# State space tables from factors that are transposed once, outputs in front of the next batch, and loads for sums requested one gate block ahead

## The chip, the cores and the metric

The kernel runs on one core of one Trainium2 chip. The metric is the device time of one execution in microseconds (us). The kernel before took 1177.91 us in the median of three runs (1176.7 to 1179.69). Its engines are called PE (TensorE, matrix products), DVE (VectorE), ACT (ScalarE), POOL (GpSimd) and SP (SyncE, which here only issues DMAs).

## The reference, cut to what matters

Two layers over 1024 tokens of width 1024. Layer 0 projects the normed input into a state space branch, a retention branch and their gates; the change touches the state space branch, which is, for each of 64 groups of 16 channels with 64 complex states:

```python
def s5_mixer(u, a_re, a_im, log_dt, b_re, b_im, c_re, c_im, d_skip, glu_w, glu_b):
    ...
    mag = jnp.exp(are * dt)
    lb_re = mag * jnp.cos(aim * dt)
    lb_im = mag * jnp.sin(aim * dt)
    ...
    bb_re = coef_re[..., None] * bre - coef_im[..., None] * bim
    bb_im = coef_re[..., None] * bim + coef_im[..., None] * bre
    ...
        y = (jnp.einsum('tbgn,ghn->tbgh', xr, cre)
             - jnp.einsum('tbgn,ghn->tbgh', xi, cim)
             + dsk * u_c)
```

Here x is the state, x(t) = lb x(t-1) + bb u(t). Then come the output projection of layer 0 and a second layer with a convolution, both untouched.

## The kernel before, in words

The program is recorded engine by engine, and a scheduler orders each engine's instructions by its own estimate of times and by the order and the holds (`issue_after`, `chained`) of the code. Large products use three products of rounded parts (`mm3`, lines 276 to 278); one half block of 128 outputs by 512 tokens is 24 of them on PE.

`layer0_front` runs on PE first eight u blocks (`u_block`, tiles `mm_u`), then sixteen gate blocks (`gate_block`, tiles `mm_g`), two half blocks each. The small work of the state space stage stands between the gate blocks: eight batches, B = 0 to 7, one for every two gate blocks. The 1024 tokens are cut into 128 pieces of 8.

- `s5_params` computes on DVE the powers of lb (`pr`, `pi`), two tables of phases (`e1`, `e2`) and the coefficients, and on POOL the matrices `bbr` and `bbi`. Its tiles come in part from the pool `ev`, which is closed before u block 5.
- `s5_tables(B)` builds on POOL, by `outer`, three pairs of 128x512 tables, six operations a pair, 18 a batch, chained in one order: M = bb times powers (`Mr`, `Mi`), the phases `Tc`, `Ts`, and W3 = powers times c. ACT makes R8.
- `s5_states(B)` loads U, transposes M on PE (tiles `w2r`, `w2i`, line 837) so that ACT can copy it to W2, multiplies U by W2 (tile `v`, line 848), rotates, scans and rotates back on DVE to the states S (lines 856 to 876). Beside that PE multiplies M by c (`kp`, lines 882 and 883), ACT copies, DVE adds dd, PE transposes (`kt`, line 888), and the result goes to DRAM (`k_d`) in rows of 128 numbers. SP loads it back as `Wd` in overlapping rows, and ACT copies that to W1.
- `s5_out(B)` makes the output y of batch B on PE from W1 and U (line 912) and from W3 and S (line 918), behind the first gate block of batch B + 1.

Also in these blocks, DVE evacuates each gate half block (`gt`, line 458), splits the weights of a later gate block (`wl_g`, line 268), and forms sums of x and of output weights for later stages (`input_sums`, `weight_sums`; tiles `xa`, `a`). All DMAs of this stage are issued by SP, in order. PSUM has three banks for the large products and five for all the others.

Of the kernel before, what the change touches and what calls it, by code (L numbers as in the profile page):

```python
# [11 lines left out]
F32 = mybir.dt.float32  # L12
# [3 lines left out]
ALU = mybir.AluOpType  # L16
# [3 lines left out]
P = 128  # L20
# [37 lines left out]
class Trunk:  # L58
# [278 lines left out]
    def layer0_front(self, st):  # L337
# [100 lines left out]
        def u_block(nb):  # L438
            ut = uv.tile([P, 8, P], F32, name=f"ut_{nb}", tag="ut", bufs=2)

            def evac(h, ps):
# [3 lines left out]
                    r.rearrange("p (m j) -> p j m", j=8), op=ALU.mult)  # L445
            if nb < 2:
                for h in range(2):
                    evac(h, u01[nb][h])
            else:
                scaled(nb, self.wnext(f"u{nb}"), f"u{nb}", evac)  # L450
            nc.sync.dma_start(self.u_d[nb].rearrange("j h g m -> (h g) j m"), ut[:])

        def gate_block(nb, w, dst):
# [8 lines left out]
            nc.sync.dma_start(dst[k * P:(k + 1) * P], gt[:])  # L462
# [123 lines left out]
    def s5_params(self, sp, tp):  # L586
# [31 lines left out]
        self.cbr, self.cbni = load("s5_cbr", (NP, 32)), load("s5_cbi", (NP, 32))  # L618
# [3 lines left out]
        v.tensor_scalar(self.cbni[:], self.cbni[:], -1.0, None, op0=ALU.mult)  # L622
# [95 lines left out]
        self.pr, self.pi = pr_, pi_  # L718

# [24 lines left out]
        grow(e2r, e2i, 7)  # L744
        self.e1 = (e1r, e1i)
# [24 lines left out]
        self.bbr, self.bbi = t((NP, 16), keep="s5_bbr"), t((NP, 16), keep="s5_bbi")  # L770
# [3 lines left out]
        gp = nc.gpsimd  # L774
        tt(x1[0], br[:], bc(cfr), ALU.mult, gp)
# [3 lines left out]
        tt(self.bbr[:], x1[0], x1[1], ALU.subtract, gp)  # L779
        tt(self.bbi[:], x1[2], x1[3], ALU.add, gp)  # L780
# [4 lines left out]
    def outer(self, B, o_r, o_i, ar, ai, br, bi, view, op_r=ALU.subtract, op_i=ALU.add):  # L785

        gp = self.nc.gpsimd
        for o, op, (a0, b0), (a1, b1) in ((o_r, op_r, (ar, br), (ai, bi)), (o_i, op_i, (ar, bi), (ai, br))):
            t = self.big(f"o_{B}", "tmpP", 2)
            yield gp.tensor_tensor(view(t[:]), a1, b1, op=ALU.mult)  # L790
            yield gp.tensor_tensor(view(o), a0, b0, op=ALU.mult)
            yield gp.tensor_tensor(o, o, t[:], op=op)

    def s5_tables(self, B):
# [6 lines left out]
        Mr, Mi = self.big(f"Mr_{B}", "Mr", 1), self.big(f"Mi_{B}", "Mi", 1)  # L801
        vm = lambda ap: ap.rearrange("p q (j h) -> p q j h", j=8)
        bj = lambda t: t[:, qs, :].unsqueeze(2).broadcast_to([P, 4, 8, 16])
        pj = lambda t, o=0: t[:, o:o + 8, qs].rearrange("p j q -> p q j").unsqueeze(3).broadcast_to([P, 4, 8, 16])
        made = [self.outer(B, Mr[:], Mi[:], bj(self.bbr), bj(self.bbi), pj(self.pr), pj(self.pi), vm)]
# [966 lines left out]
```

## Time and profile before

| | us |
|---|---|
| median of the three runs | 1177.91 |
| span of the profiled execution | 1173.9 |
| PE busy | 1161.3 |
| DVE busy | 910.5 |
| POOL busy | 713.5 |
| ACT busy | 545.1 |
| PE, eight transposes w2r and w2i of one batch, start to start | 0.79 |
| POOL, eight batches of tables | from 83.0 to 306.5 |

Of the profiled execution there is the span, from its first to its last instruction; what lies around the instructions is in the runs' times and not in the span. Durations of PE's products overlap, so the distance between two starts tells what a product costs. In the rows of the timeline a row is: start, length, engine, line, operation, output <- inputs, shape, and how many instructions were merged; a product of full 32-bit numbers that isn't a transpose counts twice (two passes). "idle before <-" names what ended an idle time.

### The profile page before, as it was taken

The page shows a single profiled execution, that of the slowest core. Times are in us where ns is not written, and L with a number is a line of the kernel's source. Part 1 is how long each engine was busy: PE and PEld are TensorE (multiplying, and loading weights), DVE is VectorE, ACT ScalarE, POOL GpSimd, SP SyncE. Part 2 cuts the span into 40 slices and gives each one's busy share as a digit, 9 for nine tenths or more (in the row PEclk, how much of TensorE's full clock was granted, in tenths as well). Part 3 has the DMA queues.
Part 4 walks back from the last instruction along what each step waited for, and adds up shares of the span by engine and source line. Part 5 has one row for each costly group of instructions (what it writes and reads, how often), then busy time and mean ns, then how long its engine had stood idle before and what let it go on. Part 6 is the DMA issues. An engine that isn't in the chain of part 4 may idle for free.

```text
span 1173.9 us, 17492 instructions
## 1 busy us (share of the span) xinstructions
PE 1161.3 (99%) x6150; PEld 965.5 (82%) x6150; DVE 910.5 (78%) x1507; ACT 545.1 (46%) x821; POOL 713.5 (61%) x507
## 2 busy tenths in 40 slices
PE   9999999999999999999999999999999999999997
PEld 7888888888888888887788888888888888888887
DVE  7875789999717475689777888479999999999643
ACT  7212343332226642123645544367756678544662
POOL 2049999888843245664444034348894689977742
PEclk9999999999999999999999999999999999999999
DMA  9353378778789765765988468965448553357863
GB/s 344 109 178 109 134 270 312 272 269 282 273 307 325 268 228 192 251 190 180 362 313 304 160 220 268 309 232 188 161 158 306 216 182 132 134 176 243 281 247 138
DMA packets 131192, 270.66 MB, mean 231 GB/s; under 512 B 12832, under 2 KB 41760, under 8 KB 130976
## 3 DMA queue, kind: packets, MB, share of 16 engines
q1 hardware_dynamic: 129952, 265.35, 66.5%
q10 hardware_dynamic: 1152, 4.19, 0.9%
q8 instruction: 48, 0.79, 0.3%
q14 instruction: 40, 0.33, 0.1%
HBM read 193.54 MB, written 71.76 MB: 226 GB/s over the span
## 4 chain that ended last, share of the span: by engine, by line
PE 91%; DMA 4%; DVE 2%; SPq 1%; ACT 1%; POOL 1%; issue 1%; DVEq 0%; POOLq 0%; ACTq 0%
PE mm_g L277 8%; PE mm_g L278 8%; PE mm_g L276 7%; PE mm_w L278 4%; PE mm_w L277 4%; PE mm_w L276 4%; PE mm_a L278 2%; PE mm_b L277 2%; PE mm_a L276 2%; PE mm_b L278 2%; PE mm_a L277 2%; PE mm_b L276 2%; PE mm_u L278 2%; PE mm_oc L278 2%; PE mm_u L277 2%; PE mm_oc L277 2%
## 5 line engine op out<-in xcount | busy, mean ns | idle before, releaser
L1461 DVE SCALAR_TENSOR_TENSOR cv<-u,convw,cv 128x512 f32<-128x512 f32 x358 | 244.7, 750 | 5.0 <-ACT cv L1447 3.5
L1441 POOL TENSOR_TENSOR tp<-tp,tp 128x512 f32<-128x512 f32 x104 | 138.9, 1338 | 28.7 <-ACT tp L1440 23.4
L278 PE MATMUL mm_g<-xh,wl_g 128*128 128x512 f32 x256 | 100.8, 394 | 0.0
L277 PE MATMUL mm_g<-xl,wh_g 128*128 128x512 f32 x256 | 100.7, 394 | 0.0
L276 PE MATMUL mm_g<-xh,wh_g 128*128 128x512 f32 x256 | 100.5, 393 | 0.0
L1440 ACT ACTIVATE tp<-u,convw 128x512 f32<-128x512 f32 x104 | 69.6, 713 | 9.6 <-POOL tp L1441 9.4
L277 PEld LDWEIGHTS mm_g<-xl,wh_g 128*128 128x128 f32 x256 | 48.1, 188 | 11.2 <-issue 1.6
L278 PEld LDWEIGHTS mm_g<-xh,wl_g 128*128 128x128 f32 x256 | 48.0, 188 | 10.5
L276 PEld LDWEIGHTS mm_g<-xh,wh_g 128*128 128x128 f32 x256 | 48.1, 188 | 9.6
L278 PE MATMUL mm_oc<-zh,wl_woc 128*128 128x512 f32 (+1 forms) x152 | 54.5, 360 | 0.2 <-DMA wl_woc<-lo_woc 0.2
L276 PE MATMUL mm_oc<-zh,wh_woc 128*128 128x512 f32 (+1 forms) x152 | 54.3, 362 | 0.0
L277 PE MATMUL mm_oc<-zl,wh_woc 128*128 128x512 f32 (+1 forms) x152 | 54.0, 357 | 0.0
L276 PE MATMUL mm_glu<-yh,wh_glu 128*128 128x512 f32 x128 | 50.0, 392 | 1.3 <-ACT sg L1250 1.3
L277 PE MATMUL mm_u<-xl,wh_u 128*128 128x512 f32 x128 | 50.1, 391 | 1.0 <-DVE xl L390 0.9
L276 PE MATMUL mm_g<-h1h,wh_cg 128*128 128x512 f32 x128 | 50.3, 393 | 0.0
L276 PE MATMUL mm_a<-h1h,wh_ca 128*128 128x512 f32 x128 | 50.3, 393 | 0.0
L278 PE MATMUL mm_b<-h1h,wl_cb 128*128 128x512 f32 x128 | 50.3, 393 | 0.0
L232 ACT CAST lh<-lf 128x512 fp32r<-128x512 f32 x32 | 19.5, 618 | 65.9 <-DMA lf<-w_c 59.3
L278 PE MATMUL mm_a<-h1h,wl_ca 128*128 128x512 f32 x128 | 50.0, 391 | 0.0
L277 PE MATMUL mm_glu<-yl,wh_glu 128*128 128x512 f32 x128 | 50.0, 392 | 0.0
L278 PE MATMUL mm_g<-h1h,wl_cg 128*128 128x512 f32 x128 | 49.9, 390 | 0.0
L277 PE MATMUL mm_g<-h1l,wh_cg 128*128 128x512 f32 x128 | 49.9, 390 | 0.0
(811 smaller groups left out, 3637.3 us busy)
## 6 DMA issues: line engine op xcount, KB each, us to landing
wf_g<-w_ab SPq DMA_DIRECT2D x16, 512.0 KB, 5.4
a<-w_out SPq DMA_DIRECT2D x32, 256.0 KB, 4.4
ws<-a SPq DMA_DIRECT2D x32, 256.0 KB, 4.8
lf<-w_c SPq DMA_DIRECT2D x32, 256.0 KB, 5.3
wf_p<-ws SPq DMA_DIRECT2D x16, 512.0 KB, 4.1
wf_cb<-w_c SPq DMA_DIRECT2D x16, 512.0 KB, 4.9
wf_ca<-w_c SPq DMA_DIRECT2D x16, 512.0 KB, 4.7
wl_cb<-lo_cb SPq DMA_DIRECT2D x16, 512.0 KB, 3.4
```

What stands on the lines that cost most here:

```text
L232: self.nc.scalar.copy(hi[:], f[:])
L276: nc.tensor.matmul(ps, wh[:, kb, :], xh, start=start, stop=False)
L277: nc.tensor.matmul(ps, wh[:, kb, :], xl, start=False, stop=False)
L278: self.last_mm = nc.tensor.matmul(ps, wl[:, kb, :], xh, start=False, stop=stop)
L1440: nc.scalar.mul(sk[:], u[:, k:k + HALF], cw[:, nb, k:k + 1])
L1441: gp.tensor_tensor(s0[:], s0[:], sk[:], op=ALU.add)
L1461: v.scalar_tensor_tensor(dst[:], *tap, accs_[i][:], op0=ALU.mult, op1=ALU.add)
```

## The change

Four things are done together.

1. **W2 is no longer transposed per batch.** Once, in front of the second half of u block 6, PE transposes the powers (`turn_p`, 4 transposes) and bb (`turn_br`, `turn_bi`, 4 each). ACT copies them and stores them to DRAM (`ptr`, `pti`, `btr`, `bti`). For each batch four DMAs of 256 KB load them, each row of 512 numbers read 16 or 8 times, as PT and BT, and POOL multiplies them to W2. M is gone. So the tables of a batch need 5 + 6 + 5 operations on POOL; phases and W3 come from three products instead of four (`outer3`), with sums and differences formed once.
2. **kp comes from W3.** W3 has 16 columns more, and kp is now the product of bb (`bblk`) with it, so it comes out already turned. The skip term dd is added by four small products with the identity. The transpose `kt` and DVE's addition are gone; ACT stores the result by eight DMAs in pieces of 16 numbers.
3. **Order.** y of batch B - 1 stands in front of v of batch B; stores of the gates, of y and of k are issued by ACT instead of SP.
4. **Loads for sums** are requested one gate block before the sums are made.

The pool `ev` is closed two u blocks later, some buffers are fewer, and two host tables of 512 KB each (`s5_cbr`, `s5_cbi`) are no longer loaded.

```diff
+                if (nb, h) == (6, 0):
+                    with tc.issue_after(self.last_mm.ins):
+                        self.s5_turned(ev)
...
-            nc.sync.dma_start(dst[k * P:(k + 1) * P], gt[:])
+            nc.scalar.dma_start(dst[k * P:(k + 1) * P], gt[:])
...
             if nb % 2 == 0:
+                if B:
+                    self.s5_out(B - 1)
                 self.s5_states(B)
-                if nb in (10, 12):
-                    with self.tc.issue_after(self.last_kg.ins):
-                        self.input_sums_made(*odd)
             gate_block(nb, self.wnext(f"g{nb}"), self.gs_d if nb < 16 else self.gr_d)
-            if nb % 2 == 0 and B:
-                self.s5_out(B - 1)
...
             with self.tc.issue_after(self.gate_evac.ins):
-                if nb in (9, 11):
-                    odd = self.input_sums(sums, nb - 9)
-                elif nb in (10, 12):
-                    self.input_sums_made(*self.input_sums(sums, nb - 9))
-                elif 13 <= nb < 21:
-                    self.weight_sums(sums, nb - 13)
+                if loaded:
+                    (self.input_sums_made if nb < 13 else self.weight_sums_made)(*loaded)
+                loaded = (self.input_sums(sums, nb - 8) if nb < 12 else
+                          self.weight_sums(sums, nb - 12) if nb < 20 else None)
...
+    def s5_turned(self, tp):
...
+        def turn(name, srcs, dsts):
+            ps = self.bank(f"turn_{name}")
+            for i, src in enumerate(srcs):
+                nc.tensor.transpose(ps[:, i * P:(i + 1) * P], src, self.ident[:])
+            t = tp.tile([P, 8, P], F32, name=f"turned_{name}", tag="xin", bufs=8)[:, :4, :]
+            self.last_turn = nc.scalar.copy(t.rearrange("p i n -> p (i n)"), ps[:])
+            n = len(srcs) // len(dsts)
+            for i, dst in enumerate(dsts):
+                nc.scalar.dma_start(dst.rearrange("(i p) n -> p i n", p=P), t[:, i * n:(i + 1) * n, :])
...
+        queue = nc.sync if B else nc.scalar
+        for t, d in zip(PT, self.pt_d):
+            queue.dma_start(t[:], bass.AP(tensor=d.tensor, offset=d.offset + qs.start * P,
+                                          ap=[[32 * P, 8], [0, 16], [1, 4 * P]]))
+        for t, d in zip(BT, self.bt_d):
+            queue.dma_start(t[:], bass.AP(tensor=d.tensor, offset=d.offset + qs.start * P,
+                                          ap=[[0, 8], [32 * P, 16], [1, 4 * P]]))
+        W2 = [self.big(f"W2{c}_{B}", f"W2{c}", 1) for c in "ri"]
+        made.append(self.outer(B, W2[0][:], W2[1][:], BT[0][:], BT[1][:], PT[0][:], PT[1][:], lambda ap: ap))
...
-            for q in range(4):
-                nc.tensor.transpose(ps[:, q * P:(q + 1) * P], M[:, q, :], self.ident[:])
...
+        made += [nc.tensor.matmul(kp[r, :P], self.bblk[0][:, q0 + q, :], W3[:, 0, q, :P], start=True, stop=False)
+                 for q, r in enumerate(rows)]
+        made += [nc.tensor.matmul(kp[r, :16], self.ident[:, r], self.dd[:, B, :], start=False, stop=False) for r in rows]
+        made += [nc.tensor.matmul(kp[r, :P], self.bblk[1][:, q0 + q, :], W3[:, 1, q, :P], start=False, stop=True)
+                 for q, r in enumerate(rows)]
...
+        for g in range(8):
+            nc.scalar.dma_start(kd[g], Kg[16 * g:16 * g + 16].rearrange("p (j o) -> p j o", j=8))
```

The order on PE, before: where the transposes of batch 4 stand (w2r and w2i), and further on the transpose kt of the same batch with the first products of y of batch 3 behind it.

```order
L277 MATMUL mm_g_1_2143<-xl_1_219,wh_g_1811 128x512
L278 MATMUL mm_g_1_2143<-xh_1_218,wl_g_1812 128x512
L837 MATMUL w2r_2227<-ident,Mr_2171 128x128 x4
L837 MATMUL w2i_2234<-ident,Mi_2172 128x128 x4
L276 MATMUL mm_g_0_2307<-xh_0_134,wh_g_2002 128x512
L277 MATMUL mm_g_0_2307<-xl_0_135,wh_g_2002 128x512
```

```order
L276 MATMUL mm_g_0_2415<-xh_0_134,wh_g_2110 128x512
L277 MATMUL mm_g_0_2415<-xl_0_135,wh_g_2110 128x512
L888 MATMUL kt_2291<-ident,Kg_2288 128x128
L912 MATMUL y_3_2363<-U_1926,W_3_1999 128x128
L912 MATMUL y_3_2364<-U_1926,W_3_1999 128x128
```

The same place of the change: the last products of y of batch 3, then v and kp of batch 4, then gate products.

```order
L973 MATMUL y_3_2277<-S_2037,W_3_1929 128x128
L973 MATMUL y_3_2278<-S_2037,W_3_1929 128x128
L904 MATMUL v_4_2306<-U_2249,W2r_2224 64x128 x8
L904 MATMUL v_4_2315<-U_2249,W2i_2225 64x128 x8
L937 MATMUL kp_2344<-W_4_2226,s_bblkr 32x128 x4
L939 MATMUL kp_2344<-s_s_dd,ident 32x16 x4
L940 MATMUL kp_2344<-W_4_2226,s_bblki 32x128 x4
L280 MATMUL mm_g_0_2378<-xh_0_134,wh_g_2075 128x512
```

From kp to the y of the next batch, 96 gate products now stand without a break; before, three groups stood between them. Only in batch 0 are v and kp still cut into pieces, with 6, 17 and 2 gate products between them.

The order on DVE in batch 5, before: the last rotation, a gate evacuation, the four weight sums (a) around a weight split (wl_g), and then the states S.

```order
L873 TENSOR_TENSOR v_5_2549<-v_5_2549,Tc_2472 128x4x127
L458 TENSOR_TENSOR gt_2605<-mm_g_1_2633,R_367 128x512
L249 TENSOR_TENSOR a_5_2693<-a_5_2691,a_5_2693 128x512
L268 TENSOR_TENSOR wl_g_2709<-wf_g_2707,wh_g_2708 128x1024
L250 TENSOR_TENSOR a_5_2695<-a_5_2695,a_5_2693 128x512
L251 TENSOR_TENSOR a_5_2697<-a_5_2697,a_5_2695 128x512
L252 TENSOR_TENSOR a_5_2691<-a_5_2691,a_5_2695 128x512
L874 TENSOR_TENSOR S_2568<-v_5_2540,d_5_2569 128x4x127
L875 TENSOR_TENSOR S_2568<-v_5_2549,d_5_2570 128x4x127
```

And of the change:

```order
L929 TENSOR_TENSOR v_5_2612<-v_5_2612,Tc_2511 128x4x127
L465 TENSOR_TENSOR gt_2674<-mm_g_0_2675,R_367 128x512
L930 TENSOR_TENSOR S_2631<-v_5_2603,d_5_2632 128x4x127
L931 TENSOR_TENSOR S_2631<-v_5_2612,d_5_2633 128x4x127
L465 TENSOR_TENSOR gt_2674<-mm_g_1_2702,R_367 128x512
L253 TENSOR_TENSOR a_5_2567<-a_5_2565,a_5_2567 128x512
L272 TENSOR_TENSOR wl_g_2748<-wf_g_2746,wh_g_2747 128x1024
```

S has moved from behind the sums and the split to a place in front of them.

The order on ACT at the end of the u blocks, before (R is the table R8, xa the input sums), and of the change, where its queue holds the stores and loads of the turned factors:

```order
L819 ACTIVATE R_1_1299<-s_s_m_480,s_r_611 128x128 x4
L267 CAST wh_g_919<-wf_g_918 128x1024
L213 ACTIVATE xa_0_1304<-xa_0_1304,vecs 128x512
L214 ACTIVATE xa_0_1306<-xa_0_1306,vecs 128x512
L213 ACTIVATE xa_1_1493<-xa_1_1493,vecs 128x512
L214 ACTIVATE xa_1_1495<-xa_1_1495,vecs 128x512
```

```order
L811 DMA ptr<-turned_p 128x2x128
L811 DMA pti<-turned_p 128x2x128
L811 DMA btr<-turned_br 128x4x128
L808 COPY turned_bi<-turn_bi 128x512
L823 COPY s_bblkr<-s_bbr 64x32x16 x2
L823 COPY s_bblki<-s_bbi 64x32x16 x2
L811 DMA bti<-turned_bi 128x4x128
L868 DMA PTr_1082<-ptr 128x1x512
L271 CAST wh_g_1022<-wf_g_1021 128x1024
L868 DMA PTi_1083<-pti 128x1x512
L871 DMA BTr_1084<-btr 128x1x512
L871 DMA BTi_1085<-bti 128x1x512
```

The copies of bb to `bblk` stand ahead of the store of bti, and the load BTi is the last of all.

More of the change, by code (lines that the diff above doesn't have):

```diff
@@ L473, in layer0_front @@
         u_block(4)
+        for nb in (5, 6):
+            u_block(nb)
         early.close()
@@ L476, in layer0_front @@
         self.s5 = self.pool("s5w", 1, stack=st)
-        for nb in range(5, 8):
-            u_block(nb)
+        u_block(7)
         self.s5_tab, self.s5_back, self.s5_last = {}, {}, None
         self.s5_tables(0)
+        loaded = None
         for nb in range(8, 24):
@@ L617, in s5_params @@
         self.cr, self.nci = load("s5_cr", (NP, 16)), load("s5_ci", (NP, 16))
-        self.cbr, self.cbni = load("s5_cbr", (NP, 32)), load("s5_cbi", (NP, 32))
+        self.bblk = [sp.tile([P, NP, 32], F32, name=f"s5_bblk{c}") for c in "ri"]
+        for b in self.bblk:
+            nc.gpsimd.memset(b[:], 0.0)
         self.dd = load("s5_dd", (8, 16))
@@ L744, in s5_params @@
         grow(e2r, e2i, 7)
+        self.e2s = t((8, NP), keep="s5_e2s")
+        self.e1s = t((17, NP), keep="s5_e1s")
+        tt(self.e2s[:], e2r[:], e2i[:], ALU.add)
+        tt(self.e1s[:], e1r[:], e1i[:], ALU.add)
+        self.last_phase = tt(e1i[:], e1i[:], e1r[:], ALU.subtract)
         self.e1 = (e1r, e1i)
@@ L769, in s5_params @@
             tt(cfi[:], a1[:], rden[:], ALU.mult)
-        self.bbr, self.bbi = t((NP, 16), keep="s5_bbr"), t((NP, 16), keep="s5_bbi")
+        self.bbr, self.bbi = (tp.tile([P, 16, NP], F32, name=f"s5_bb{c}") for c in "ri")
         bc = lambda q: q[:].unsqueeze(2).broadcast_to([P, NP, 16])
@@ L778, in s5_params @@
         tt(x1[3], br[:], bc(cfi), ALU.mult, gp)
-        tt(self.bbr[:], x1[0], x1[1], ALU.subtract, gp)
-        tt(self.bbi[:], x1[2], x1[3], ALU.add, gp)
+        tt(self.bbr[:].rearrange("p h q -> p q h"), x1[0], x1[1], ALU.subtract, gp)
+        tt(self.bbi[:].rearrange("p h q -> p q h"), x1[2], x1[3], ALU.add, gp)
+    def s5_turned(self, tp):
+        nc = self.nc
+        self.pt_d = [self.dram.tile([8, 32, P], F32, name=f"pt{c}") for c in "ri"]
+        self.bt_d = [self.dram.tile([16, 32, P], F32, name=f"bt{c}") for c in "ri"]
+        def turn(name, srcs, dsts):
[7 more added lines that the diff above has]
+                nc.scalar.dma_start(dst.rearrange("(i p) n -> p i n", p=P), t[:, i * n:(i + 1) * n, :])
+        fl = lambda t: t.rearrange("p a b -> p (a b)")
+        cols = lambda t, n: [fl(t)[:, i * P:(i + 1) * P] for i in range(n)]
+        rows = lambda d: d[:].rearrange("a b n -> (a b) n")
+        turn("p", cols(self.pr[:, 0:8, :], 2) + cols(self.pi[:, 0:8, :], 2), [rows(d) for d in self.pt_d])
+        for c, b in zip("ri", (self.bbr, self.bbi)):
+            turn(f"b{c}", cols(b[:], 4), [rows(self.bt_d["ri".index(c)])])
+        for blk, b in zip(self.bblk, (self.bbr, self.bbi)):
+            for g in range(2):
+                r = slice(64 * g, 64 * g + 64)
+                with self.tc.issue_after(self.last_turn.ins):
+                    nc.scalar.copy(blk[r, :, 16 * g:16 * g + 16], b[r].rearrange("p h q -> p q h"))
@@ L825, in s5_states @@
         q0 = 4 * B
[L826 to L840 removed]
+        U, W2, W3, Tc, Ts, R8 = self.s5_tab.pop(B)
         V = []
@@ L854, in s5_states @@
         vr, vi = V[0][:], V[1][:]
-        t2, t4 = (fl(self.big(f"m{i}_{B}", "tmpV", 4)) for i in range(2))
+        t2, t4 = (fl(self.big(f"m{i}_{B}", "tmpV", 2)) for i in range(2))
         v.tensor_tensor(t2, vi, ts, op=ALU.mult)
@@ L868, in s5_states @@
         zr, zi = (z.rearrange("p (q n) -> p q n", q=4) for z in (vr, vi))
-        t2, t3 = (self.big(f"d{i}_{B}", "tmpV", 4) for i in range(2))
+        t2, t3 = (self.big(f"d{i}_{B}", "tmpV", 2) for i in range(2))
         v.tensor_tensor(c0(t2), c0(zi), c0(Ts), op=ALU.mult)
```

84 lines of the change are left out of this document (40 added, 44 removed).

## The prediction

> **What bounds the kernel now.** I read three views in this order: the page's busy times, the waits of TensorE, and the windows over the state space stage.
>
> ```profile
> PE 1161.3 (99%) x6150; PEld 965.5 (82%) x6150; DVE 910.5 (78%) x1507; ACT 545.1 (46%) x821; POOL 713.5 (61%) x507
> PE mm_glu L276 <- ACT sg L1250: 1.3, 1, 1.3
> PE idle L366 <- DVE epst L311: 1.1, 1, 1.1
> ```
>
> PE is busy 99% of the span, and the two longest waits of PE in the whole program are 1.3 and 1.1 us. No engine keeps PE waiting, so the time is the PE instruction stream. Two kinds of edit can move it: instructions taken from or added to that stream, and new waits.
>
> ```profile
> 156.00:185.50 29.50, 29.50 (x203) 24.69 (x202) 25.98 (x31) 10.54 (x19) 26.95 (x19) 1.00 0.75 265
> 185.50:215.00 29.50, 29.50 (x203) 24.69 (x202) 28.26 (x32) 9.80 (x19) 27.33 (x20) 1.00 0.86 302
> 215.00:244.50 29.50, 29.50 (x203) 24.69 (x202) 27.43 (x30) 9.20 (x18) 25.82 (x19) 1.00 0.75 264
> 244.50:274.00 29.50, 29.50 (x203) 24.69 (x202) 27.33 (x30) 9.19 (x18) 25.74 (x19) 1.00 0.81 278
> 274.00:303.50 29.50, 29.50 (x203) 24.68 (x202) 27.36 (x30) 8.03 (x14) 25.74 (x19) 1.00 0.80 276
> L837 PE MATMUL w2r<-ident,Mr x32: 269/272/273, 100.9 to 303.8; 128*128 128x128 f32 x32
> ```
>
> The columns are stretch, length, then busy time and count of PE, PEld, DVE, ACT and POOL, granted clock, DMA share, GB/s. The first transposes of the eight batches start from 100.9 to about 303.5 us, seven periods, so one period is 28.9 us on average; from batch 1 on it is 29.5 us, and PE fills it at clock 1.00. DVE fills 27.4 us of it, POOL 25.7 us, ACT 9 us.
>
> **What the change takes from PE.** One batch, in order of time, in three places:
>
> ```profile
> 126.21 0.39 PE L278 MATMUL mm_g<-xh,wl_g 128*128 128x512 f32 x1
> 126.44 0.60 PE L837 MATMUL w2r<-ident,Mr 128*128 128x128 f32 x4
> 126.88 0.60 PE L837 MATMUL w2i<-ident,Mi 128*128 128x128 f32 x4
> 127.23 0.47 PE L276 MATMUL mm_g<-xh,wh_g 128*128 128x512 f32 x1
> 127.55 0.40 PE L277 MATMUL mm_g<-xl,wh_g 128*128 128x512 f32 x1
> ...
> 132.12 0.39 PE L276 MATMUL mm_g<-xh,wh_g 128*128 128x512 f32 x1
> 132.44 1.09 PE L848 MATMUL v<-U,W2r 128*64 128x128 f32 x16
> 133.36 1.04 PE L848 MATMUL v<-U,W2i 128*64 128x128 f32 x16
> 134.34 0.45 PE L882 MATMUL kp<-Mr,s_s_cbr 128*32 128x128 f32 x8
> 134.58 0.42 PE L883 MATMUL kp<-Mi,s_s_cbi 128*32 128x128 f32 x8
> 134.93 0.50 PE L277 MATMUL mm_g<-xl,wh_g 128*128 128x512 f32 x1
> 135.27 0.39 PE L278 MATMUL mm_g<-xh,wl_g 128*128 128x512 f32 x1
> ...
> 141.19 0.39 PE L277 MATMUL mm_g<-xl,wh_g 128*128 128x512 f32 x1
> 141.42 0.27 PE L888 MATMUL kt<-ident,Kg 128*128 128x128 f32 x1
> 141.53 1.95 PE L912 MATMUL y<-U,W 128*128 128x128 f32 x16
> 143.40 2.06 PE L918 MATMUL y<-S,W 64*128 64x128 f32 x32
> 145.39 0.50 PE L278 MATMUL mm_g<-xh,wl_g 128*128 128x512 f32 x1
> 145.73 0.40 PE L276 MATMUL mm_g<-xh,wh_g 128*128 128x512 f32 x1
> ```
>
> Starts count here, since durations overlap. From 127.55 to 132.12 lie 20 gate products: 4.57 / 20 = 0.228 us each. The list of terms:
>
> 1. The eight transposes w2r and w2i: from 126.21 to 127.55 are 1.34 us for two product steps; less 2 x 0.228 that leaves 0.88 us. They go in all 8 batches: **-7.0 us**.
> 2. The transpose kt: 141.53 - 141.42 = 0.11 us, 8 times: **-0.9 us**.
> 3. Small products stand in two further groups, v with kp, and kt with y. After the change y, v and kp are one group. Going in from a product costs 0.32 instead of 0.23 us (132.12 to 132.44), coming back 0.34 (134.93 to 135.27), so a group has 0.1 to 0.2 us of its own. One group less in 7 batches, at 0.15: **-1.0 us**.
> 4. The four products of ident with dd (16 columns, two passes each, 8 passes a batch). No row shows 16 columns. The nearest is kp: 16 passes from 134.34 to 134.93, 0.037 us a pass, so at most 8 x 0.037 = 0.30 us; in proportion to the columns it would be 0.04 us. A pass has a part that doesn't shrink with the columns, so I take 0.2 us, nearer the row: **+1.6 us** (0.3 to 2.4). The kp products themselves keep number and shape and change their order, from pairs on one 32-column strip to four strips in turn: taken as 0, bounded by half of their 0.59 us either way, -2.4 to +2.4 us.
> 5. Batch 0 is cut differently (v in two halves, kp in two pieces): three more groups at 0.2: **+0.6 us**.
> 6. Twelve transposes once, in front of the second half of u block 6, at 0.88 / 8: **+1.3 us**.
>
> Sum: -7.0 - 0.9 - 1.0 + 1.6 + 0.6 + 1.3 = **-5.4 us**.
>
> On term 4 a page takes a side: the Trainium skill, "TensorEngine Tiling (Array Packing)", section Performance Considerations, says that a matmul has some 60 cycles of overhead, so that a free dimension of 1 takes as long as one of 60. By that, the 16 columns would not be cheaper in proportion; at the 2.4 GHz that the Trainium skill, "Trainium Kernel Development and Optimization", section Quick Reference, gives for TensorE, that is an estimated 25 ns a pass, 0.2 us a batch, and the same sum. By the opposite, pure proportion, the sum would be -6.7 us. No run here shows the 16 columns.
>
> **What hides the rest.** Everything else moves between engines that PE doesn't wait for; I checked the three ends that PE will wait on in a steady batch. T is the start of v; the next y is due 1.90 (v) + 0.59 + 0.2 + 96 x 0.228 = 24.6 us later.
>
> ```profile
> 223.04 0.69 DVE L856 TENSOR_TENSOR m<-v,Ts 128x512 f32<-128x512 f32 x1 [0.74 <-PE v L848]
> 242.15 0.67 DVE L875 TENSOR_TENSOR S<-v,d 128x508 f32<-128x508 f32 x1
> L934 ACTq DMA_DIRECT2D yn_d<-yn x8: 326/362/389, 364.7 to 417.6; - x8
> k_d<-Kt SPq DMA_DIRECT2D x5, 64.0 KB, 1.5
> DMA to landing us min/median/max: 3.9/5.1/6.2
> L897 ACT COPY W<-Wd x8: 1049/1052/1053, 124.1 to 337.2; 128x1024 f32<-128x1024 f32 x8
> ```
>
> - S: before, DVE needed 223.04 to 242.8 = 19.8 us with a weight split and four sums inside; now S stands ahead of them. Even the old 19.8 us, and 2 us for v, end 2.8 us early.
> - W1: the copy of kp, then 8 stores issued by ACT at 0.36 = 2.9 us, the landing, Wd (5.1 us to landing) and the copy of 1.05 us: 0.3 + 2.9 + 1.5 + 5.1 + 1.05 = 10.9 us from kp's end, with some 22 us there. The stores are of 64 bytes where before they were of 512; the landing may be 11 us longer before PE notices. The Trainium skill, "DMA: Bandwidth & Descriptors", section Specifications, asks for transfers of at least 512 B, below which a write becomes read and write; it gives no price, and were the 1.5 us landing doubled or tripled, the sum would not move.
> - W2 for the next batch: POOL waits for v, since W2 has one buffer, then makes six operations of 1.1 to 1.3 us, about 7.5 us of the 28.8 us until the next v. POOL has 16 operations a batch instead of 18. The loads of PT and BT wait only for the W2 before.
>
> ACT gets 11 issues at 0.36 = 4 us a batch and loses two copies of 0.58: 9 + 3 of 28.8 us. On DVE the small addition goes, and the period shrinks: 27.4 of 28.8 us. If that cover fails, DVE becomes the bound of the stage at once, and each us it lacks costs 8 us in all.
>
> **The start**, the one place with little cover. The tables of batch 0 now go PE, ACT, DRAM, SBUF, POOL.
>
> ```profile
> 84.35 0.39 PE L278 MATMUL mm_u<-xh,wl_u 128*128 128x512 f32 x1
> 76.17 0.19 DVE L607 TENSOR_TENSOR s_cfi<-s5t,s5t 128x32 f32<-128x32 f32 x1
> 81.64 1.29 POOL L607 TENSOR_TENSOR s_bbi<-s5bb 128x512 f32<-128x512 f32 x1
> 83.01 1.11 POOL L790 TENSOR_TENSOR o<-s_bbi,s_pi 128x512 f32<-128x512 f32 x1
> 101.88 0.58 ACT L839 COPY W2r<-w2r 128x512 f32<-128x512 f32 x1
> DMA to landing us min/median/max: 3.2/3.8/7.7
> ```
>
> The last line is u_d's. The first half of u block 6 ends at 84.6, so the turning begins there and its last four transposes at 85.5. bbi was there at 82.9; DVE now has about 0.8 us more ahead of cfi, and the two last POOL operations write across, at worst twice 1.29: 83.7 to 86.3. I take no wait, bound 0 to 0.8 us. Then W2r is due after 72 u and 22 gate products: 85.9 + 94 x 0.228 = 107.3, W2i at 109.7. The supply: three copies of 0.58 and three issues bring ACT to 87.9, four block copies at some 0.6 to 90.3, then the store of bti, landing 3.8 later at about 94.6, the load of BTi, landing at 98.8, three POOL operations to 102.5 (W2r), three to 106.2 (W2i). That is 3.5 us early at the median landing; with both transfers at 7.7 us it is 4 us late.
>
> **The forecast**: the profiled execution's span of 1173.9 us becomes 1168.5; the median of the runs, 1177.9, is 4.0 us above that span, and I keep that: 1177.9 - 5.4 = **1172.5 us** (-0.46%).
>
> **Rivals.**
> (a) *A late start table.* PE waits at the first v for W2. For it: ACT's queue puts the store of bti behind four copies, and the load of BTi behind it. Against: 3.5 us of cover at median landings, and a lightly used DMA there. Price at the slowest landings 4 us: 1172.5 + 4 = 1176.5 us, no change that can be seen. Chance 0.15.
> (b) *The DMA engines fill up*: slower. From 156 to 303.5 us the five rows average 277 GB/s at a share of 0.79, so about 349 GB/s when full, 10.05 MB in 28.8 us. The stage moves 277 x 29.5 = 8.17 MB a batch and gets 4 x 262 KB = 1.05 MB more: share 0.92, still below one, on average. It decides from the point where reading one 2 KB row 8 or 16 times costs 1.8 times its face value. At 2.3 times it is 10.6 MB, 30.3 us a batch, 1.5 over; six batches give +9 and the end is 1172.5 + 9 = 1181.5 us. The first sign would be late sums on DVE, which stand in front of the gate evacuations. For it: 0.86 in one row already. Against: loads are asked for a block ahead, the old share is an average with room in four rows of five, and input sums are spread over four blocks instead of two pairs. Chance 0.15.
> (c) *The order of kp and the fixed part cost what they can*: the sum with both upper bounds, and the wait at the turning, is -5.4 + 0.8 + 2.4 + 0.8 = -1.4: 1176.5 us. It is the upper end of my forecast, not a case apart. The lower end is -5.4 - 1.3 - 2.4 = -9.1: 1168.8 us.
>
> **Chances.** A measurement here can tell about 0.3% (3.5 us) from no change, so faster means below 1174.4. The forecast (1168.8 to 1176.5) has 0.70, of which 0.10 lies above 1174.4; (a) 0.15 and (b) 0.15. Faster 0.60, same 0.25, slower 0.15. The range takes in the forecast's own bounds and (a), and part of (b): 1168.5 to 1179.
>
> **What would show it.** Right: the windows of the steady batches shrink to 28.6 to 28.9 us with PE full; no w2 or kt rows; twelve turn rows at 0.11 us from about 84.6; TensorE's waits name neither W2, S, W nor gt. Wrong: a PE wait at the first v on POOL W2 (a); DVE rows that wait for DMA a, and a DMA share near 1.00 (b); PE waiting for W<-Wd, if the stores of 64 bytes land late. A period shorter than 28.4 us would mean that kp or dd cost less than their rows. Outside 84 to 348 us the order on PE is nearly the same, so the 12.6 us in which PE isn't busy should stay within 1 or 2 us; a larger difference there would also make me wrong.

## The result and the profile after

| | before | after |
|---|---|---|
| median of the runs, us | 1178.07 (4 runs) | 1205.95 (4 runs, 1205.32 to 1208.06) |
| ratio, 95% interval | | 1.0237 (1.0219 to 1.0255) |
| span of the profiled execution, us | 1173.9 | 1203.6 |
| mean granted clock of PE | 0.999 | 0.988 |

The kernel is 2.4% slower; the forecast was 0.46% faster. The busy times on the page of the kernel after:

```profile
PE 1165.3 (97%) x6154; PEld 968.1 (80%) x6154; DVE 898.9 (75%) x1502; ACT 542.1 (45%) x820; POOL 691.5 (57%) x495
```

PE is busy 4.0 us more than before, but for 97% of the span instead of 99%. Its waits, with total, number and longest in us:

```profile
PE y L967 <- ACT W L952: 21.3, 4, 7.6
PE mm_glu L280 <- ACT sg L1305: 2.5, 1, 2.5
```

A wait has appeared that the forecast took to be covered: the products y wait for W1, four times, 21.3 us in all (7.6, 7.1, 4.4 and 2.1). The windows over the state space stage (columns as in the prediction) show that PE loses more than that:

```profile
140.00:200.00 60.00, 49.47 (x328) 41.02 (x325) 45.40 (x52) 15.27 (x32) 55.90 (x40) 0.91 0.76 240
200.00:260.00 60.00, 55.67 (x387) 47.35 (x388) 43.89 (x55) 16.00 (x32) 43.35 (x32) 0.94 0.86 282
260.00:320.00 60.00, 53.46 (x366) 45.31 (x365) 41.45 (x55) 12.62 (x25) 35.78 (x28) 0.91 0.84 279
...
164.00:168.00 4.00, 1.67 (x8) 1.68 (x9) 2.72 (x4) 2.77 (x4) 3.84 (x4) 0.50 1.00 206
168.00:172.00 4.00, 4.00 (x34) 3.77 (x35) 3.96 (x3) 0.27 (x1) 3.92 (x3) 0.58 0.69 245
172.00:176.00 4.00, 4.00 (x74) 3.38 (x71) 3.96 (x5) 0.72 (x1) 3.84 (x3) 1.00 0.88 241
```

The granted clock, 1.00 in the steady batches before, is 0.91 to 0.94 here. The second group is the neighbourhood of the wait that ended at 166.33: after it the clock is 0.50 until 171.3, though PE is busy (the window with 0.58 holds the return to 1.00). Behind the other three waits it is 0.50 for 4.5, 6.0 and 3.2 us of work. A stall so costs twice. The timeline of PE shows both, and one batch without a stall:

```profile
204.33 3.79 PE L967 MATMUL y<-U,W 128*128 128x128 f32 x16 [7.09 <-ACT W L952]
208.04 2.44 PE L973 MATMUL y<-S,W 64*128 64x128 f32 x32
210.41 1.09 PE L904 MATMUL v<-U,W2r 128*64 128x128 f32 x16
...
212.31 0.42 PE L937 MATMUL kp<-W,s_bblkr 128*32 128x128 f32 x8
212.55 0.23 PE L939 MATMUL kp<-s_s_dd,ident 128*32 128x16 f32 x8
212.61 0.41 PE L940 MATMUL kp<-W,s_bblki 128*32 128x128 f32 x8
...
234.85 1.95 PE L967 MATMUL y<-U,W 128*128 128x128 f32 x16
236.74 2.06 PE L973 MATMUL y<-S,W 64*128 64x128 f32 x32
238.72 1.09 PE L904 MATMUL v<-U,W2r 128*64 128x128 f32 x16
...
240.92 0.41 PE L940 MATMUL kp<-W,s_bblki 128*32 128x128 f32 x8
```

The same sixteen products take 3.79 us behind a wait of 7.09 us, and 1.95 us without one. The batch from v at 210.41 to v at 238.72 has no stall and takes 28.31 us, against 29.5 us for a steady batch before and 28.6 to 28.9 forecast. So PE's own stream did get shorter. Where the time is lost, one row for each kernel shows: the first products of the first `mm_q`, behind the state space stage (count up to 520 us, shortest, median and longest in ns, first and last start). First before:

```profile
L276 PE MATMUL mm_q<-xh,wh_q x53: 387/390/505, 347.7 to 519.7; 128*128 128x512 f32 x53
```

and after:

```profile
L280 PE MATMUL mm_q<-xh,wh_q x40: 387/389/504, 374.2 to 516.3; 128*128 128x512 f32 x40
```

26.5 of the 29.7 us between the spans are lost ahead of this place. By the forecast `mm_q` would start at 347.7 - 5.4 = 342.3; the stage is 31.9 us late against that, of which the waits name 21.3, 0.7 (v for W2i) and 0.6 (the turning). The other 9 us go with the clock: 5.0, 4.5, 6.0 and 3.2 us of work at half rate are an estimated 9.4 us lost. PE's busy time says the same: the forecast's -5.4 and these 9.4 make the 4.0 us that it has more.

Why is W1 late? The waits of SP's DMA queue between 140 and 320 us, first before, then after:

```profile
SPq L244 <- DMA ws<-a: 19.2, 19, 3.2
SPq L892 <- ACT Kt L890: 13.2, 6, 3.5
```

```profile
SPq L243 <- DMA ws<-a: 43.0, 22, 4.5
SPq L950 <- DMA k_d<-Kg: 18.6, 6, 4.6
```

Added over all rows of this view (26 before, 31 after), SP waited 33.6 us for landings of DMAs and 75 us for engines before; after, it waits 107.9 us for landings and 10 us for engines. **The stage was paced by engines and is now paced by transfers.** On ACT, one batch after (ACTq rows are DMA issues):

```profile
244.34 0.36 ACTq L979 DMA_DIRECT2D y_d<-yb  x1
244.79 0.27 ACT L944 COPY Kg<-kp 128x128 f32<-128x128 f32 x1 [4.61 <-DMA ws<-a]
248.06 7.50 ACTq L947 DMA_DIRECT2D k_d<-Kg  x8
255.61 1.28 ACT L886 ACTIVATE R<-s_s_m,s_r 128x128 f32<-128x128 f32 x4 [10.55 <-DMA k_d<-Kg]
...
266.63 1.04 ACT L952 COPY W<-Wd 128x1024 f32<-128x1024 f32 x1 [7.75 <-DMA Wd<-k_d]
```

The program counts the DMAs of both queues on eight completion semaphores in turn, so that an issue can wait for an older DMA on the same one. Here the store of y on ACT waits for a store `ws` that SP issued, the copy of Kg stands behind it, and the eight pieces take 7.50 us to issue, such waits included. On SP, in the same batch, the loads of PT and BT stand ahead of the load of Wd, which then waits until the pieces have landed:

```profile
256.50 0.58 SPq L871 DMA_DIRECT2D BTi<-bti  x1
261.34 0.38 SPq L950 DMA_DIRECT2D Wd<-k_d  x1
```

In the batch before, the same gap is from 224.1 to 227.9 us, and since 221.2 us neither queue had issued anything but these loads and pieces of K. SP stands still for transfers, and yet the DMA share in the gap is only 0.48, at 150 GB/s. What keeps the loads at half is a question to the runs below.

### The profile page after: what moved, and what is told of

Its sections match the earlier page's. It is cut to its first block, busy times and chain, and to the rows that moved or that the text cites. A ratio compares the mean times of both kernels' runs of the same rounds, so it can differ in the third digit from the quotient of the medians.

```text
span 1203.6 us, 17599 instructions
## 1 busy us (share of the span) xinstructions
PE 1165.3 (97%) x6154; PEld 968.1 (80%) x6154; DVE 898.9 (75%) x1502; ACT 542.1 (45%) x820; POOL 691.5 (57%) x495
## 4 chain that ended last, share of the span: by engine, by line
PE 68%; DMA 12%; DVE 3%; issue 1%; SPq 1%; ACT 1%; ACTq 0%; POOL 0%; DVEq 0%; POOLq 0%
PE mm_w L282 4%; PE mm_w L280 4%; PE mm_w L281 4%; PE mm_g L280 4%; PE mm_g L282 4%; PE mm_g L281 4%; DMA ws<-a 3%; PE mm_a L282 2%; PE mm_a L280 2%; PE mm_b L282 2%; PE mm_b L280 2%; PE mm_b L281 2%; PE mm_a L281 2%; PE mm_oc L282 2%; PE mm_oc L281 2%; PE mm_oc L280 2%
## 5 line engine op out<-in xcount | busy, mean ns | idle before, releaser
L1496 POOL TENSOR_TENSOR tp<-tp,tp 128x512 f32<-128x512 f32 x104 | 138.7, 1336 | 28.8 <-ACT tp L1495 23.6
L280 PEld LDWEIGHTS mm_g<-xh,wh_g 128*128 128x128 f32 x256 | 48.0, 188 | 10.9 <-issue 1.2
L272 DVE TENSOR_TENSOR wl_g<-wf_g,wh_g 128x1024 fp32r<-128x1024 f32 x16 | 25.7, 1605 | 36.8 <-ACT wh_g L271 36.8
L166 ACT CAST wh_p<-wf_p 128x1024 fp32r<-128x1024 f32 x28 | 29.5, 1053 | 47.6 <-PE mm_w L281 38.7
L280 PE MATMUL mm_u<-xh,wh_u 128*128 128x512 f32 x128 | 49.6, 398 | 0.6 <-ACT wh_u L271 0.4
```

Source lines behind the costliest of these rows:

```text
L166: self.nc.scalar.copy(wh[:].rearrange(fl), wf[:])
L272: lo[i].tensor_tensor(wl[:].rearrange(fl)[:, c], wf[:, c], h.bitcast(F32), op=ALU.subtract)
L280: nc.tensor.matmul(ps, wh[:, kb, :], xh, start=start, stop=False)
L1496: gp.tensor_tensor(s0[:], s0[:], sk[:], op=ALU.add)
```

## The experiments

Times are medians; the kernel before ran on the same chip each time, at 1177.1 to 1178.4. Letters: the theories A to A4 say that single parts of the change make W1 late, B that the stage is short of transfer rate.

**One part undone at a time.** e1, y behind the first gate block again:

```diff
-                if B:
-                    self.s5_out(B - 1)
                 self.s5_states(B)
             gate_block(nb, self.wnext(f"g{nb}"), self.gs_d if nb < 16 else self.gr_d)
+            if nb % 2 == 0 and B:
+                self.s5_out(B - 1)
```

> The changed kernel with the output products y put back where the kernel before had them, behind the first gate block of the next batch (about 11 us of gate products later); nothing else is undone. Theory A (PE loses its time only because W1 arrives after the place where y now stands, and the granted clock falls as a consequence of that wait): the latest W1 is 7.6 us late and the new place is 11 us later, so PE has no wait over 1 us on W at y, the granted clock in 140-320 us is back above 0.97, and the time is 1205.95 - 21.3 (waits) - 13.5 (clock) + 1.0 (one group more in seven batches) = 1172, between 1170 and 1176. Rival B (the added traffic and its shared completions are the bound, W1 only shows it): the wait is moved, W1 comes later still or v waits for W2, and the time stays above 1190.

Measured 1204.45 us (1.0218, 1.0195 to 1.0240). W1 is in time, and the wait is elsewhere. PE's longest waits in e1:

```profile
PE v L904 <- DMA U<-u_d: 20.2, 4, 9.0
PE kp L940 <- POOL W L845: 2.7, 2, 1.5
```

Rival B holds: 20.2 us at v for U in place of 21.3 us at y for W1. The others gave the same picture. e2:

```diff
+                if nb in (10, 12):
+                    with self.tc.issue_after(self.last_kg.ins):
+                        self.input_sums_made(*odd)
...
-                if loaded:
-                    (self.input_sums_made if nb < 13 else self.weight_sums_made)(*loaded)
-                loaded = (...)
+                if nb in (9, 11):
+                    odd = self.input_sums(sums, nb - 9)
+                elif nb in (10, 12):
+                    self.input_sums_made(*self.input_sums(sums, nb - 9))
+                elif 13 <= nb < 21:
+                    self.weight_sums_made(*self.weight_sums(sums, nb - 13))
```

> The changed kernel with the sums of x and of weights loaded and made as in the kernel before (same block, and for two of them behind the copy of Kg); y stays in front. Theory A2 (the two waits of 7.6 and 7.1 us come from activations on ACT that wait 2 to 7 us for x loads ahead of the copy of Kg, the others from elsewhere): the waits at the first two steady batches shrink to under 3 us, the ones of 4.4 and 2.1 us stay, and the time is about 1206 - 10 (waits) - 6 (clock) = 1190, between 1183 and 1196. Rival (the order on ACT only hides a late landing of the eight pieces; it is the pieces): the first two waits stay above 5 us each and the time is within 3 us of 1206.

Measured 1207.83 us; the waits at y are 17.0 us in five places. e3:

```diff
-            nc.scalar.dma_start(dst[k * P:(k + 1) * P], gt[:])
+            nc.sync.dma_start(dst[k * P:(k + 1) * P], gt[:])
...
-        nc.scalar.dma_start(self.y_d[B].rearrange("i h g m -> (i h) g m"), yb[:])
+        nc.sync.dma_start(self.y_d[B].rearrange("i h g m -> (i h) g m"), yb[:])
```

> The changed kernel with the stores of y and of the gates issued on SP again instead of ACT; all else as changed. Theory A3 (ACT's own DMA issues couple the copy of Kg to landings; from the third steady batch on, the copy waits about 5 us behind the issue of the y store): the waits of 4.4 and 2.1 us go, those of 7.6 and 7.1 us stay, and the time is about 1206 - 6.5 - 4 = 1195, between 1190 and 1200. Rival (SP, which is in order too, then holds the load of Wd behind a store that waits for a gate): the wait at y grows in all batches and the time is above 1206.

Measured 1205.68 us; waits at y 21.8 us. e4:

```diff
-        kd = self.k_d[B, 112:].rearrange("(j i) (g o) -> g i j o", j=8, g=8)
-        for g in range(8):
-            nc.scalar.dma_start(kd[g], Kg[16 * g:16 * g + 16].rearrange("p (j o) -> p j o", j=8))
+        kp = self.bank(f"kt_{B}")
+        nc.tensor.transpose(kp[:, :P], Kg[:], self.ident[:])
+        Kt = w.tile([P, P], F32, name=f"Kt_{B}", tag="Kg", bufs=1)
+        nc.scalar.copy(Kt[:], kp[:, :P])
+        nc.scalar.dma_start(self.k_d[B, 112:], Kt[:])
```

> The changed kernel with K transposed on PE again and stored by one DMA (on ACT's queue) instead of eight; y stays in front. Theory A4 (the eight pieces with their issue of 4 to 9.5 us and their landing one behind the other are the largest part of W1's lateness): W1 is 4 to 7 us earlier less 1 us for transpose and copy, the waits fall from 21.3 to under 8 us, and with the clock and 0.9 us of transposes the time is about 1206 - 14 - 9 + 1 = 1184, between 1177 and 1192. Rival (the queue ahead of Kg on ACT decides; the pieces cost little): the waits change by less than 5 us in sum and the time is above 1198.

Measured 1207.30 us; 15.0 us at y and 5.6 us at kt. Theories A to A4 fall as single causes. e8 makes the edits of e1 to e3 at once, and e13 those of e1 and e4:

> The changed kernel with all three changes of order undone at once: y behind the first gate block, sums loaded and made as in the kernel before, gate and y stores on SP. What stays of the change is PT and BT and the eight pieces of K. Theory B: the stage is held by its transfers in any order, so 1200 to 1207 and SP's waits for DMAs above 85 us in 140-320 us. Rival (the orders compensate each other when undone one at a time): under 1185.

> The changed kernel, PT and BT loaded as it does, with K transposed on PE and stored by one DMA and y behind the first gate block: the two parts that each bring the run with plain rows from 1188 to under 1180, here with the loads left as they are. Theory B3 (the loads on half of the DMA engines, and of the same rows, are enough to bind the stage): 1197 to 1206, with the waits moved to U or W2. Rival (the loads matter only while the pieces or the early y need them out of the way): 1176 to 1188.

Measured 1201.03 (two runs) and 1201.37 us. As long as PT and BT are loaded as the change loads them, no order and no form of K's store brings more than 5 us.

**The loads.** e5 loads PT and BT for batch 0 only; e6 does so with PT alone:

```diff
-        for t, d in zip(PT, self.pt_d):
+        for t, d in zip(PT, self.pt_d) if not B else ():
...
-        for t, d in zip(BT, self.bt_d):
+        for t, d in zip(BT, self.bt_d) if not B else ():
```

> The changed kernel, but PT and BT are loaded for batch 0 only and used for all batches (left out: 28 loads of 262 KB; W2 of batches 1 to 7 is made of batch 0's factors, and the state space output is wrong from there). Theory B (the transfers of PT and BT are what the stage waits for; they hold SP's queue at landings): SP's waits for DMAs in 140-320 us fall from 108 us to under 60, PE's waits at y to under 3 us in sum, and the time is 1172 to 1178. Rival (the eight pieces, the order on ACT and SP, or the place of y, each covering for the other): the waits stay, and the time is above 1195.

> The changed kernel, but PT alone is loaded for batch 0 only; BT is loaded in each batch (left out: 14 loads of 262 KB; wrong from batch 1 on). Theory B with a price in proportion: half of what the run without both gains, so 1186 to 1193. With a threshold (the queue copes until it is full): nearly all of the gain, under 1180. Rival (PT and BT are not the cause): 1203 to 1207.

Measured 1192.04 (1.0127, 1.0103 to 1.0152) and 1202.61 us (two runs), outside of every range given. Without the loads 14 us come back: less than theory B said, and half of the loads cost most of it. e7 keeps the bytes and reads other rows; e9 and e10 take apart what is particular about the rows. e9, for PT and for BT:

```diff
-                                          ap=[[32 * P, 8], [0, 16], [1, 4 * P]]))
+                                          ap=[[0, 16], [32 * P, 8], [1, 4 * P]]))
...
-                                          ap=[[0, 8], [32 * P, 16], [1, 4 * P]]))
+                                          ap=[[32 * P, 16], [0, 8], [1, 4 * P]]))
```

e7, and then e10, in place of the loads of PT and BT:

```diff
+            queue.dma_start(t[:].rearrange("p q n -> p (q n)"), self.A["xT"][2 * i + B % 2, :, :HALF])
...
+            queue.dma_start(t[:], bass.AP(..., ap=[[17 * T, 8], [T, 16], [1, 4 * P]]))
```

> The changed kernel, but the four loads of PT and BT of each batch read 128 different rows of 2 KB of x (same bytes, same packets, same queue, same place) instead of 8 or 16 rows many times over; W2 is then made of x, and the state space output is wrong. Theory B1 (reading the same rows again and again costs more than their bytes, the 1.8 times named in the prediction): the loads land sooner, the waits at y mostly go, and the time is 1172 to 1182. Theory B2 (it is the bytes and the four places in SP's queue, whatever is read): 1198 to 1206, the waits as before.

> The changed kernel, but the loads of PT and BT name their outermost dimension as 16 instead of 8: PT reads each of 8 rows 16 times as 16 groups of 8 (the rows then lie in the wrong partitions), BT each of 16 rows 8 times as 16 groups of 8. Same DRAM rows, same number of reads of each, same bytes and places in the queue; W2 is made of misplaced factors and the state space output is wrong. Theory B3 (a load whose outermost dimension is 8 runs on 8 of the 16 DMA engines, half as fast; the Trainium skill, DMA: Bandwidth & Descriptors, section on why a DMA increments its semaphore by 16, says so): as fast as from plain rows, 1185 to 1191. Theory B1 (reading one row many times is what is slow): 1202 to 1207, as before.

> The counterpart: the four loads read 128 different rows of x, in 8 groups of 16 with a step between groups that lets the outermost dimension stay 8 (W2 is made of x; the state space output is wrong). Theory B3 (engines): 1201 to 1207, as with PT and BT. Theory B1 (repeated rows): 1185 to 1191, as from plain rows.

| us (ratio's interval) | 128 different rows | 8 or 16 rows, many times |
|---|---|---|
| outermost dimension 16 or 128 | e7 1188.17 (1.0055 to 1.0108) | e9 1197.73 (1.0166 to 1.0196) |
| outermost dimension 8 | e10 1201.39 (1.0146 to 1.0248) | after 1205.95 (1.0219 to 1.0255) |

Both properties cost: 13.2 us for the eight alone, 9.6 us for the equal rows alone, 17.8 us together. B1 and B3 were put as alternatives, and e9's time lies between their ranges. e10's four runs spread from 1191.9 to 1205.3, so its share is the less certain one: its interval meets that of the kernel after, and what the equal rows add to the eight is not clear of noise. What an outermost dimension of 8 does, e18 shows by accident. It was to put the four loads of a batch into the kernel before:

```diff
+        d = self.A["xT"][0]
+        for i in range(4 if B else 0):
+            t = self.big(f"X{i}_{B}", f"X{i}", 1)
+            nc.sync.dma_start(t[:], bass.AP(...
+                                            ap=([[0, 8], [32 * P, 16]] if i // 2 else [[32 * P, 8], [0, 16]]) + [[1, 4 * P]]))
```

> The kernel before, computing as it did, with four more loads of 262 KB on SP in batches 1 to 7, in the place and the form that the change gives PT and BT (8 rows 16 times, 16 rows 8 times, outermost dimension 8), read from x into four tiles that nothing uses; to make room, three tags have the smaller numbers of buffers that the change gives them. Theory B3 (these loads alone take the room that the transfers had): the waits on DMA appear on SP, PE waits in the state space stage, and the time is 1188 to 1204. Rival (the kernel before has room for them, and it takes the change's order or the pieces to bind): 1177 to 1182.

Measured 1199.61 us, but not for the reason expected: nothing used the tiles, so nothing held the loads back. SP issued all 28 between 82 and 138 us, the first v behind waited 17.0 us for W2r, once, and from 200 to 380 us PE was busy all the time. It doesn't tell whether the loads alone bind a steady batch. It does show a stretch with such loads only. The DMA busy share in 40 slices of 121 to 133 us, in tenths, and what they moved:

```profile
DMA  5554545545455454555744454555555555555555
GB/s 205 178 164 157 198 184 205 198 184 198 178 198 212 184 198 184 205 191 198 246 164 177 164 191 171 191 191 191 198 198 198 198 191 198 191 198 198 198 198 198
```

and the window's row, with the share in the last column but one:

```profile
121.00:133.00 12.00, 11.46 (x55) 9.24 (x53) 2.22 (x4) 0.63 (x1) 11.53 (x10) 1.00 0.52 192
```

With loads queued all the time the share stays at 0.52, at 192 GB/s. Counted packet by packet in the trace, 8 to 11 packets are under way at every moment of this stretch, 8 of them in 68% of it, which fits half of the engines at work all the time, and not all of them half the time. From 224.1 to 227.9 us of the kernel after the count is the same: 8 to 11, 8 in 67%. The Trainium skill, "DMA: Bandwidth & Descriptors", section "Why a DMA increments its semaphore by 16 and not by 1", has the rule: a DMA issued by SP or ACT uses as many engines as the largest number up to 16 that divides the outermost sizes of both its access patterns, the lowest-numbered ones; its rules for authors name a leading broadcast of c copies. PT's and BT's patterns begin with 8. The trace agrees on the half: 0.52. Which engines these are, it doesn't show.

**What is left with plain rows.** 1188.17 us is still 15.7 above the forecast. e11 and e12 add e4's and e1's edit to e7:

> Plain rows of x for PT and BT, and K transposed on PE and stored by one DMA (W2 is made of x; wrong output of the state space). What of the 1188.2 us with plain rows is still above the forecast, 1188.2 - 1172.5 = 15.7 us, should be the eight pieces by theory A4: they hold SP's Wd load, and what stands behind it, until they have landed (12.4 and 7.5 us in 140-320 us). By it 1173 to 1179. Rival (with 1.05 MB a batch more the stage is still short of transfer rate, pieces or not): 1184 to 1189.

> Plain rows of x for PT and BT, and y behind the first gate block (W2 is made of x; wrong output of the state space). Theory A (once the transfers keep up on average, the place of y decides: 9.0 us of waits at y with plain rows, 5.3 us the longest, and 11 us more room): 1188.2 - 9.0 - about 4 of clock + 1 = 1176, between 1173 and 1180. Rival (the wait moves to U or W2 as it did with y later alone): 1184 to 1189.

Measured 1177.14 us (1.0006, 0.9993 to 1.0019) and 1179.37 us (1.0013, 1.0002 to 1.0024). Either one is enough: with transfers that keep up, the pieces are only late for a y that stands in front. And between e4 (1207.30) and e11, and between e1 (1204.45) and e12, only the loads of PT and BT differ, at the same bytes: 30.2 and 25.1 us, the clearest sign that the form of these loads is the cause. e11's windows:

```profile
140.00:200.00 60.00, 58.56 (x452) 48.73 (x453) 56.52 (x64) 20.32 (x42) 58.12 (x39) 1.00 0.88 306
200.00:260.00 60.00, 59.28 (x413) 49.69 (x412) 59.04 (x65) 18.27 (x39) 54.98 (x38) 1.00 0.93 311
260.00:320.00 60.00, 59.59 (x414) 49.64 (x413) 43.63 (x58) 15.19 (x28) 35.73 (x27) 1.00 0.88 299
```

299 to 311 GB/s go through at clock 1.00, more than the 240 to 282 after. The bytes of the change are not the limit. Are the PE terms right? e14 (no loads, both edits) and e17 (no loads, e4's edit):

> PT and BT loaded for batch 0 only, K transposed on PE and stored by one DMA, y behind the first gate block (left out: 28 loads; W2 of batches 1 to 7 is made of batch 0's factors). Nothing then asks more of the transfers than the kernel before did, so the time shows the PE terms of the prediction alone: 1172.5 + 0.9 (kt) + 1.0 (one group more) = 1174.4, between 1172 and 1177. Rival (a PE term was wrong too, or the sums loaded ahead and the stores on ACT cost by themselves): above 1179.

> As e14, but y stays in front: PT and BT loaded for batch 0 only, K transposed on PE and stored by one DMA (left out: 28 loads). e14 came out 9 us above the forecast, with PE waiting 2.7 us for W2i and 2.5 us for W3 on POOL; W3 has two buffers and y frees one, so a later y may hold POOL. Theory (that is the price of the later y once the transfers are out of the way): no wait on POOL above 1.5 us, and 1172.5 + 0.9 = 1173.4, between 1172 and 1178. Rival (a PE term was wrong, or the rest of the change costs by itself): 1180 to 1186 as e14.

Measured 1183.53 (1180.48 to 1188.27) and 1185.19 us (1181.8 to 1190.4); both forecasts missed. e17's profile shows why, first in ACT's timeline:

```profile
224.54 0.26 ACT L878 COPY W<-s_s_ci 128x64 f32<-128x64 f32 x1
229.39 0.36 ACTq L981 DMA_DIRECT2D y_d<-yb  x1
229.85 0.27 ACT L944 COPY Kg<-kp 128x128 f32<-128x128 f32 x1 [5.06 <-DMA ws<-a]
```

and at the first products of `mm_q`:

```profile
L280 PE MATMUL mm_q<-xh,wh_q x48: 387/389/504, 351.5 to 508.1; 128*128 128x512 f32 x48
```

The issue of y's store on ACT waits until 229.39 for a landing of `ws`, Kg stands behind it, and PE waits for Kg at kt: 5.6 us in two places, and the clock falls to 0.97 for 60 us (1.8 us). With 342.3 + 0.9 for kt, 0.9 for W2i at v and 0.5 at the turning that is 352.0 us, against 351.5 in the row: the sum of PE's own terms holds within 0.5 us in this run, which is the fastest of the six. Why this coupling bites without the loads and not in e11 is open; e14 has its waits on POOL instead (2.7 us for W2i, 2.5 us for W3). e5, without the loads, is slower than e7 with plain rows as well (1192.04 and 1188.17), so a run that leaves the loads out doesn't give their price cleanly.

**A kernel that computes the same.** e15 and e16 store BT eight times and PT twice in DRAM, at the turning, and load from there, e15 with e4's edit and e16 with e1's. Shown are the copies of BT, then the loads of PT and of BT:

```diff
+            for i in range(4):
+                nc.sync.dma_start(x[:, i].rearrange("j p n -> p j n"), t[:, i, :].unsqueeze(1).broadcast_to([P, 8, P]))
...
+                                              ap=[[32 * P, 16], [0, 8], [1, 4 * P]]))
...
+                                              ap=[[32 * P, P], [1, 4 * P]]))
```

> A version that computes the same: BT is stored eight times and PT twice in DRAM (once, at the turning, 4.7 MB more by twelve and eight DMAs on SP), so that for batches 1 to 7 BT's loads read 128 different rows and PT's name 16 groups of 8 equal rows; K transposed on PE and stored by one DMA. Theory B3: near the run with plain rows and turned K (1177.1) plus up to 5 us for PT's equal rows: 1177 to 1183. Rival (the copies' 4.7 MB fall into the start, where the first W2 has 3.5 us to spare): above 1184, with a wait at the first v.

> The same spread loads with K in eight pieces and y behind the first gate block. Theory B3: near the run with plain rows and y later (1179.4) plus up to 5 us: 1179 to 1185. Rival as for the run before: above 1186, with a wait at the first v.

Measured 1206.94 and 1206.62 us, in the range of the rival. SP's queue in e15:

```profile
87.63 6.66 SPq L827 DMA_DIRECT2D bxr<-turned_br  x4
94.39 7.50 SPq L827 DMA_DIRECT2D bxi<-turned_bi  x4
...
109.47 0.62 SPq L458 DMA_DIRECT2D u_d<-ut  x1
```

The copies hold SP from 87 to 109 us, u_d's store and all loads stand behind them, and PE waits 7.9 us at a v for W2r. That is not all: e15 also waits 12.1 us at y for W1, in three places, and e16 9.5 us at v for W2i and Ts. What holds these was not followed, so these two runs don't decide about the spread loads. No version here beats the kernel before.

## Why the prediction was wrong, point by point

- **"PE doesn't wait for" the rest** is the step that failed, and in it W1: "10.9 us from kp's end, with some 22 us there". In the batch shown kp ended at 240.92 + 0.41 = 241.33, and W1 was there at 266.63 + 1.04 = 267.67: 26.3 us, for a y that was due after 22.0 and waited 4.41. Kg was copied 3.7 us after kp's end where 0.3 was taken, since the queue ahead of it on ACT (4.61 us of idle time) was put at nothing. The first piece left 3.0 us after that copy, and the eight issues, put at 8 x 0.36 = 2.9 us, took 7.50. From there to the issue of Wd were 5.8 us, where a landing of 1.5 was taken. Wd's own 5.3 us and the copy's 1.04 were as forecast (5.1 and 1.05). "PE waiting for W<-Wd" did stand in the list of signs, but for the landing of the small pieces, which e4 shows not to be the cause by itself.
- **Rival (b), "the DMA engines fill up"**, is the mechanism, with a chance of 0.15 and mis-sized. The forecast spread the 1.05 MB over 16 engines and came to a share of 0.92. On eight engines, these carry 8.17 / 2 + 1.05 = 5.13 MB where they had 4.08: an estimate from the forecast's own rows is 0.79 x 29.5 / 28.8 x 5.13 / 4.08 = 1.02. By that they are full, while the mean over 16 stays at 0.76 to 0.86 and looks harmless; no view shows the share of a single engine. The point of decision, "1.8 times its face value", was passed: half the engines alone make it 2. But (b) gave 1181.5 us, since it priced the transfer only, not the stalls and the clock that follow. Its signs were the wrong ones: over the stage the share is not near 1.00, and DVE's waits from 84 to 350 us name no DMA. SP's waits for landings were the right one.
- **Terms 1 to 6** hold in their sum: 374.2 less the waits (21.3, 0.7 and 0.6) and 9.4 of clock is 342.2 us for `mm_q`, against 342.3; e17 agrees within 0.5 us. In e11, 342.3 + 0.9 for kt and waits of 1.6, 0.9 and 0.5 make 346.2, and `mm_q` began at 347.4. Term 4 was too high: from the dd products to the next is 212.61 - 212.55 = 0.06 us, near proportion (0.04) and not the 0.2 taken. The Trainium skill's 60 cycles a matmul ("TensorEngine Tiling (Array Packing)", Performance Considerations), by which it would have been an estimated 0.2 us, do not show in this sum. The four products go to four different strips of 32 columns; no run here tells what products on one strip would take. "A period shorter than 28.4 us would mean that kp or dd cost less than their rows": it is 28.31.
- **The start**: PE waited 0.6 us at the turning, within 0 to 0.8, and 0.7 us for W2i. Rival (a) didn't come.
- **Outside the stage**: "within 1 or 2 us"; 3.2 us were lost behind the start of `mm_q`. Of them 1.2 are a longer wait of `mm_glu` for sg (2.5 us, 1.3 before) and 1.0 a new wait of `mm_q`; the rest was not looked for.

## What to carry to other kernels

A mean DMA share below one is no room: look at which engines a transfer can use (its outermost dimension) and at what the issuing queue waits for, engines or landings. When a change replaces engine work by loads, price the loads on the engines that carry them. When undoing parts one at a time changes nothing, look for a resource under all of them; here the wait only moved from W1 to U.

## What was not expected of the hardware

- Loads whose pattern begins with 8 ran at 192 GB/s and a DMA share of 0.52, back to back (e18). In e7, loads of different rows and a store reached 389 GB/s together at a share of 1.02 (173 to 177 us).
- Reading the same 8 or 16 rows many times costs 9.6 us over seven batches even with an outermost dimension of 16 (e9 against e7). Why was not tried, and e18 speaks against a slower engine: its loads read equal rows too, and 192 / (16 x 0.52) = 23 GB/s a busy engine is no less than 277 / (16 x 0.79) = 22 in the kernel before.
- After a stall of PE of 7.6 us the granted clock was 0.50 for 5.0 us more of busy time. The Trainium skill, "TensorE: Matmul & The Clock Gate", Part 1, describes this gate, half rate after an idle window of about 3.4 us. The trace agrees on the half rate, 0.50, but not on the length: a wait of 2.1 us was followed by it too (301.2 us), and one of 2.5 us (606 us) was not.
